# Weights and small parameters of a hybrid attention, S5, mLSTM and MoE layer laid out in the order of their tiles

## The chip, the cores and the metric

The kernel runs on one core of a Trainium2 chip. The metric is the device time of one execution in microseconds (us). The layouts of the inputs are made by numpy before the launch, and that is outside the time.

## The reference

One transformer-like layer with batch 1, 256 tokens and width 2048, all in float32. Shift, scale and gate vectors come from `silu(c) @ w_ada + b_ada`, a product of one row with a 2048 x 12288 matrix. The modulated, normalized input goes through `w_in` (2048 x 14344). The result is cut into the operands of three mixers (stick-breaking attention, an S5 state space layer, a chunkwise mLSTM) and their gates. Each mixer's output is projected, the gated sum goes through `w_out`, and after a second norm comes a mixture of 32 experts in 4 groups.

```python
mod = c_act @ w_ada[l] + b_ada[l]
h = modulate(rms_norm(x, norm_mix_g[l]), shift1, scale1)
proj = h @ w_in[l]
...
merged = jax.nn.sigmoid(g_sb) * (y_sb @ p_sb[l]) \
    + jax.nn.sigmoid(g_s5) * (y_s5 @ p_s5[l]) \
    + jax.nn.sigmoid(g_ml) * (y_ml @ p_ml[l])
x = x + gate1[:, None, :] * (merged @ w_out[l])
...
hid = jax.nn.silu(jnp.einsum('td,edf->tef', t, w1)) * jnp.einsum('td,edf->tef', t, w3)
y = jnp.einsum('tef,efd->td', hid * gates.astype(hid.dtype)[:, :, None], w2)
```

Of the experts each token uses two, but all 32 experts' matrices (2048 x 256 twice and 256 x 2048 each) are read. Some 480 MB are read in one execution, nearly all of them weights, each once.

## The kernel before

All weights are streamed through SBUF in tiles of 128 partitions by 2048 floats (1 MB, 8 KB per partition). Nearly all loads are issued from SP's queue.

**Start.** SP loads `c` (L94) and the two halves of `x` (L73); POOL loads the first constants (L96), the first part of `b_ada` (L98) and `norm_mix_g` (L100), both in pieces of four floats. `norm_x` (L366 on) normalizes `x` on ACT. `ada_pe(0)` (L309) streams the first eighth of the used part of `w_ada`: eight tiles, each of two transfers of 512 KB (L321, one for shift and one for scale, rows of 512 floats), multiplied on PE (L327) into `adarp`. The ring for these tiles has three buffers. Their sum becomes the shift and scale of the first 512 channels (`ada_cols`), with which `hT_block` makes the first modulated block hT; then the first matmuls of `w_in` (tile `u_w`) run.

**Early columns.** A loop over four blocks of 512 rows runs ten column chunks of `w_in` per block (u, sbq, sbk, sbv, mlq, mlk), while `ada_first` (L288) streams the next block's `w_ada` tiles, whose products DVE accumulates (L301, L303).

**Main part.** `ChanChunk` and `TokChunk` take a weight tile of 512 rows and 512 columns through `wsplit`: `load_raw` (L118, ring of three buffers) loads it, ACT rounds it to fp32r in two halves (L131), DVE makes the remainder (L132), and PE multiplies three times (`mm3`, L142 to L144). The order of the chunks is that of the program: the rest of `w_in` for the mixers, then its gate columns (g_sb, g_ml, g_s) alternating with the projections p_sb, p_ml, p_s5, then w_out. In the background DVE runs the S5 recurrence (L695 to L698) and the remaining two thirds of `w_ada` (`ada_rest`, L337; tile `adar`, also through L118; DVE L353). `rows4` and `rows_kp` (L252, L255) give the source of each tile: 4 rows of 2 KB per partition, either neighbouring ones or 128 rows apart.

**Experts.** A `Pair` (L1357 on) is two experts that share PE's columns, half 0 and half 1. `load_in` (L1372) loads for each of four blocks of 512 rows and each expert a tile with 4 KB of w1 and 4 KB of w3 per partition, in two transfers (L1377); `load_out` (L1383) loads w2 in tiles of 8 KB rows (L1391). The ring has eleven buffers. PE multiplies w1 and w3 into `h` and w2 into `y` (both L1397); between them come gathers of the next tokens (xg, xgT), the scatter of the last ones (sc), and for `h` a silu on ACT (L1409), a product on DVE (L1410) and a transpose.

Except in blocks marked `manual_schedule`, the framework writes each engine's queue when the kernel is built: by priority among the instructions that it takes to be ready. So the order in a queue can differ from the program's.

```python
def rows4(mat, c0):
    return lambda j: mat[512 * j:512 * j + 512, c0:c0 + 512].rearrange("(p k) c -> p k c", k=4)
...
for wi, nm in enumerate(("moe_w1", "moe_w3")):
    nc.sync.dma_start(out=raw[:, wi], in_=A[nm][e, 512 * j:512 * j + 512, :]
                      .rearrange("(p k) f -> p k f", k=4))
```

Of the kernel before, what the change touches and what calls it, by code (L numbers as in the profile page):

```python
# [10 lines left out]
F32 = mybir.dt.float32  # L11
# [7 lines left out]
P = 128  # L19
D = 2048  # L20
T = 256
W = 1024
NE = 32
FF = 256
# [4 lines left out]
CONST_COLS = 6 * 128 + 2 + 16 + 12  # L29
# [15 lines left out]
def kernel(ctx: ExitStack, tc: tile.TileContext, A, out, dbg=None):  # L45
# [43 lines left out]

    def cols4(v):  # L90
        return v.rearrange("(j p k) -> p j k", p=P, k=4)
# [9 lines left out]
    gmoe = cp.tile([P, 4, 4], F32, name="gmoe")  # L101
    ccol = cp.tile([P, 4, 4], F32, name="ccol")
# [185 lines left out]
    def ada_first(j):  # L288
        acc = pbp.tile([P, 2, 512], F32, tag="acc", bufs=1, name=f"acc{j}")
        for jr in range(4):  # L290
            for kp in range(2):
                raw = pap.tile([P, 2, 2, 512], F32, tag="raw", bufs=3, name=f"ada{j}_{jr}_{kp}")
                for v in range(2):
                    c0 = v * D + 512 * j
                    nc.sync.dma_start(out=raw[:, v], in_=A["w_ada"][512 * jr:512 * jr + 512, c0:c0 + 512]
                                      .rearrange("(p k) c -> p k c", k=4)[:, 2 * kp:2 * kp + 2, :])
                with tc.high_priority(120):
                    for q in range(2):
                        cs = ccol[:, jr, 2 * kp + q:2 * kp + q + 1]
                        if jr == 0 and kp == 0 and q == 0:  # L300
                            nc.vector.tensor_scalar(acc, raw[:, :, q], cs, None, op0=ALU.mult)  # L301
                        else:
                            nc.vector.scalar_tensor_tensor(acc, raw[:, :, q], cs, acc, op0=ALU.mult, op1=ALU.add)  # L303
                    if jr == 3 and kp == 1:
                        ada_cols(modc[:, 0:2, 4 * j:4 * j + 4], ball[:, j:j + 5:4, :],
                                 ada_rows([acc[:, v] for v in range(2)], f"f{j}"), f"f{j}")
                yield

    def ada_pe(j):  # L309
# [6 lines left out]
        for jr in range(4):  # L316
            for kp in range(2):
                raw = pap.tile([P, 2, 2, 512], F32, tag="raw", bufs=3, name=f"ada{j}_{jr}_{kp}")
                for v in range(2):
                    c0 = v * D + 512 * j  # L320
                    nc.sync.dma_start(out=raw[:, v], in_=A["w_ada"][512 * jr:512 * jr + 512, c0:c0 + 512]  # L321
                                      .rearrange("(p k) c -> p k c", k=4)[:, 2 * kp:2 * kp + 2, :])
                for kk in range(2):
# [13 lines left out]
    def ada_rest():  # L337
        cols = []
        for v in (2, 3, 4, 5):
            for half in range(2):  # L340
                acc = pbp.tile([P, 1024], F32, tag="acc", bufs=1, name=f"accr{v}_{half}")
                for n in range(16):
                    jr, kp, q = n // 4, n // 2 % 2, n % 2
                    if q == 0:
                        c0 = v * D + 1024 * half
# [63 lines left out]
    def s5_params():  # L409
# [114 lines left out]
        br, bi, ta, tb = (cut(512 * i, 32, 16) for i in range(4))  # L524
        nc.gpsimd.dma_start(out=br, in_=A["s5_b_re"].rearrange("(j g) p h -> (g p) j h", g=2))
        nc.gpsimd.dma_start(out=bi, in_=A["s5_b_im"].rearrange("(j g) p h -> (g p) j h", g=2))
        bc = cut(2048, 2, 32, 16)
# [41 lines left out]
        for r, nm in enumerate(("s5_c_re", "s5_c_im")):  # L569
            cc = cut(0, 8, 64)  # L570
            nc.gpsimd.dma_start(out=cc, in_=A[nm].rearrange("(u g) h p -> (g h) u p", g=8))
            cx = cut(512, 8, 2, 64)
# [173 lines left out]
    def gates_chunk():  # L746
        wif = pap.tile([P, 2, 2, 512], F32, tag="raw", bufs=3, name="wif")[:, 0, 0, :128].rearrange("p (k c) -> p k c", k=16)
        for j in range(4):
            nc.gpsimd.dma_start(out=wif[:, 4 * j:4 * j + 4, :],
                                in_=A["w_in"][512 * j:512 * j + 512, COL["gates"]:COL["gates"] + 8]  # L750
                                .rearrange("(p k) c -> p k c", k=4))
        ws = p1.tile([P, 2, T], F32R, tag="sby", name="wifs")
# [198 lines left out]
    for j in range(4):  # L951
# [12 lines left out]
        if j == 2:  # L964
            nc.sync.dma_start(out=cst[:, 256:], in_=A["consts"][:, 256:])
            nc.sync.dma_start(out=ball[:, 8:], in_=cols4(A["b_ada"])[:, 8:])
            nc.sync.dma_start(out=gmoe, in_=cols4(A["norm_moe_g"]))
        if j == 3:
# [393 lines left out]
    class Pair:  # L1362
# [220 lines left out]
    def overflow():  # L1583
# [3 lines left out]
        with tc.If(nmax > 64):  # L1587
# [9 lines left out]
            for tt in range(2):  # L1597
# [12 lines left out]
                for e in range(NE):  # L1610
                    ph = psum("ms", f"ho{tt}_{e}")
                    for j in range(4):
                        raw = st.tile([P, 2048], F32, tag="raw", bufs=3, name=f"o13_{tt}_{e}_{j}")
                        rv = raw.rearrange("p (w k f) -> p w k f", w=2, k=4)
                        for wi, nm in enumerate(("moe_w1", "moe_w3")):
                            nc.sync.dma_start(out=rv[:, wi], in_=A[nm][e, 512 * j:512 * j + 512, :]
                                              .rearrange("(p k) f -> p k f", k=4))
                        for kk in range(4):
# [136 lines left out]

_SHAPES = dict(
    x=(T, D), c=(D,), norm_mix_g=(D,), norm_moe_g=(D,), final_g=(D,), w_ada=(D, 6 * D), b_ada=(6 * D,),
    w_in=(D, 14344), ml_conv=(4, 2 * W), ml_i_bias=(4,), ml_f_bias=(4,), s5_lam_re=(64, 64), s5_lam_im=(64, 64),
    s5_log_dt=(64,), s5_b_re=(64, 64, 16), s5_b_im=(64, 64, 16), s5_c_re=(64, 16, 64), s5_c_im=(64, 16, 64),
    s5_d=(W,), s5_w_glu=(W, W), p_sb=(W, D), p_s5=(W, D), p_ml=(W, D), w_out=(D, D), moe_w_group=(D, 4),  # L1760
    moe_b_group=(4,), moe_w_router=(D, 32), moe_b_router=(32,), moe_w1=(NE, D, FF), moe_w3=(NE, D, FF),
    moe_w2=(NE, FF, D))

# [17 lines left out]
```

## Time and profile before

| | us |
|---|---|
| median of 3 runs | 1601.37 |
| lowest and highest | 1597.33, 1603.7 |
| profiled execution, its time | 1600.31 |
| span of its profile | 1598.5 |

The span runs from the first to the last instruction of the profiled execution; 1.81 us of that execution's time lie around it. By the profile's page the time falls into three stretches: a start without much matmul work up to about 40 us, the part from there to about 1093 us in which weights are split and multiplied, and the experts from 1093 us to about 1580 us. The page's engines are PE (matmul), PEld (weight load), DVE, ACT, POOL and SP. Busy time of PE includes modelled ends of pipelined matmuls, so what PE waits for says more than its share.

### The profile page before, as it was taken

To read this page: it belongs to the slowest core of one execution; us is meant where nothing else is said; L and a number is where in the kernel's file an instruction comes from. 1 tells how busy PE (TensorE), PEld (TensorE's weight loads), DVE (VectorE), ACT (ScalarE), POOL (GpSimd) and SP (SyncE) were. 2 spreads that over 40 slices of the span, in tenths; PEclk is the share of its full clock that TensorE was granted. 3 is DMA by queue.
4 is the path that set the end of the run, shared out by engine and by line. 5 is a ranking of instruction groups with operands and counts; after the bars stand their busy time and mean duration, and the time that the engine had idled before them with its cause. 6 is when DMAs were issued, how large, how long until landed. Compare 5 with 4: busy or idle time off the path is not lost.

```text
span 1598.5 us, 25021 instructions
## 1 busy us (share of the span) xinstructions
PE 1509.0 (94%) x10228; PEld 1140.2 (71%) x10228; DVE 1015.1 (64%) x1733; ACT 568.6 (36%) x755; POOL 39.0 (2%) x63
## 2 busy tenths in 40 slices
PE   4999999989999998999999999999999999999996
PEld 2999999888888988899999998874334433443332
DVE  0879997889879999999778866553213212222124
ACT  3554363774534333333444344342112111111112
POOL 1000010010000000000000010000000000000000
PEclk9999999999999999999999999999999999999998
DMA  9998967677787676777789976566999999999994
GB/s 343 386 348 305 319 191 222 220 223 261 247 300 265 229 264 231 273 264 264 263 308 327 318 267 241 207 228 257 414 413 412 413 402 374 412 392 411 404 412 183
DMA packets 172249, 488.13 MB, mean 305 GB/s; under 512 B 13876, under 2 KB 14048, under 8 KB 162784
## 3 DMA queue, kind: packets, MB, share of 16 engines
q1 hardware_dynamic: 168464, 473.27, 80.5%
q0 software_dynamic: 3088, 12.14, 2.3%
q8 instruction: 82, 1.34, 0.3%
q10 hardware_dynamic: 576, 1.05, 0.2%
q14 instruction: 39, 0.32, 0.1%
HBM read 479.06 MB, written 6.31 MB: 304 GB/s over the span
## 4 chain that ended last, share of the span: by engine, by line
PE 54%; DVE 25%; DMA 10%; issue 6%; ACT 4%; POOL 0%; SPq 0%; ACTq 0%; DVEq 0%; POOLq 0%
PE h L1397 14%; PE y L1397 9%; DVE accr L353 5%; DMA adar<-in_w_ada_dram 4%; DVE g_sb_w L132 2%; DVE g_ml_w L132 2%; PE sc L1446 2%; PE wo_b L143 2%; PE wo_b L144 2%; PE wo_b L142 2%; DVE bu L698 2%; PE xg L1312 2%; DVE s5pp L695 2%; DVE bu L697 1%; DVE s5qq L696 1%
## 5 line engine op out<-in xcount | busy, mean ns | idle before, releaser
L1397 PE MATMUL h<-w,XG 128*64 128x512 f32 x1024 | 245.3, 599 | 0.0
L1397 PEld LDWEIGHTS h<-w,XG 128*64 128x64 f32 x1024 | 75.7, 137 | 139.1 <-issue 137.4
L353 DVE SCALAR_TENSOR_TENSOR accr<-adar,ccol,accr 128x1024 f32<-128x1024 f32 x120 | 153.5, 1280 | 18.2 <-DMA adar<-in_w_ada_dram 17.3
L1397 PE MATMUL y<-w,hh 128*64 128x512 f32 x512 | 150.4, 598 | 0.5 <-ACT hh L1419 0.5
L1410 DVE SCALAR_TENSOR_TENSOR s<-h,gg,s 128x256 f32<-128x256 f32 x16 | 7.7, 484 | 167.8 <-ACT s L1409 167.8
L1455 DVE TENSOR_TENSOR x<-x,sc 128x512 f32<-128x512 f32 x64 | 43.0, 682 | 105.7 <-PE sc L1446 105.7
L1397 PEld LDWEIGHTS y<-w,hh 128*64 128x64 f32 x512 | 49.0, 136 | 81.5 <-issue 77.7
L1409 ACT ACTIVATE s<-h 128x256 f32<-128x256 f32 x16 | 6.1, 383 | 212.3 <-PE h L1397 212.3
L144 PE MATMUL g_sb_b<-hT,g_sb_w 128*128 128x256 f32 x256 | 73.1, 285 | 8.5 <-DVE g_sb_w L132 8.4
L144 PE MATMUL g_ml_b<-hT,g_ml_w 128*128 128x256 f32 x256 | 72.4, 283 | 3.3 <-DVE g_ml_w L132 3.3
L1287 DVE TENSOR_SCALAR XG<-xgT,G,modc 128x128 f32<-128x128 f32 x64 | 26.0, 410 | 77.0 <-ACT XG L1284 77.0
L144 PE MATMUL g_s_b<-hT,g_s_w 128*128 128x256 f32 x256 | 72.1, 282 | 1.6 <-DVE g_s_w L132 1.4
L142 PE MATMUL g_ml_b<-hT,g_ml_w 128*128 128x256 f32 x256 | 72.4, 283 | 0.0
L142 PE MATMUL g_sb_b<-hT,g_sb_w 128*128 128x256 f32 x256 | 71.9, 281 | 0.0
L142 PE MATMUL g_s_b<-hT,g_s_w 128*128 128x256 f32 x256 | 71.7, 280 | 0.0
L143 PE MATMUL g_s_b<-hT,g_s_w 128*128 128x256 f32 x256 | 71.6, 280 | 0.0
L143 PE MATMUL g_ml_b<-hT,g_ml_w 128*128 128x256 f32 x256 | 71.5, 279 | 0.0
L143 PE MATMUL g_sb_b<-hT,g_sb_w 128*128 128x256 f32 x256 | 71.4, 279 | 0.0
L132 DVE TENSOR_TENSOR wo_w<-wo_w,wo_w 128x1024 fp32r<-128x1024 f32 x32 | 39.0, 1223 | 31.8 <-ACT wo_w L131 31.6
L303 DVE SCALAR_TENSOR_TENSOR acc<-ada,ccol,acc 128x1024 f32<-128x1024 f32 x45 | 57.6, 1281 | 0.5
L131 ACT CAST g_ml_w<-g_ml_w 128x1024 fp32r<-128x1024 f32 x32 | 32.0, 1048 | 70.4 <-DMA g_ml_w<-in_w_in_dram 47.4
L144 PEld LDWEIGHTS g_sb_b<-hT,g_sb_w 128*128 128x128 f32 x256 | 48.1, 188 | 11.2 <-DVE g_sb_w L132 11.1
(506 smaller groups left out, 4361.7 us busy)
## 6 DMA issues: line engine op xcount, KB each, us to landing
w<-in_moe_w_dram SPq DMA_DIRECT2D x256, 512.0 KB, 9.2
adar<-in_w_ada_dram SPq DMA_DIRECT2D x64, 1024.0 KB, 5.5
w<-in_moe_w_dram SPq DMA_DIRECT2D x64, 1024.0 KB, 9.9
ada<-in_w_ada_dram SPq DMA_DIRECT2D x64, 512.0 KB, 7.5
g_sb_w<-in_w_in_dram SPq DMA_DIRECT2D x16, 1024.0 KB, 5.4
g_ml_w<-in_w_in_dram SPq DMA_DIRECT2D x16, 1024.0 KB, 5.4
g_s_w<-in_w_in_dram SPq DMA_DIRECT2D x16, 1024.0 KB, 6.1
wo_w<-in_w_out_dram SPq DMA_DIRECT2D x16, 1024.0 KB, 5.1
```

Source lines behind the costliest of these rows:

```text
L131: nc.scalar.copy(out=hv, in_=src)
L132: nc.vector.tensor_tensor(out=lv, in0=src, in1=hv.bitcast(F32), op=ALU.subtract)
L142: nc.tensor.matmul(o, lhsT=lhs[0], rhs=rhs[0], start=start, stop=False, **kw)
L143: nc.tensor.matmul(o, lhsT=lhs[0], rhs=rhs[1], start=False, stop=False, **kw)
L144: nc.tensor.matmul(o, lhsT=lhs[1], rhs=rhs[0], start=False, stop=stop, **kw)
L303: nc.vector.scalar_tensor_tensor(acc, raw[:, :, q], cs, acc, op0=ALU.mult, op1=ALU.add)
L353: nc.vector.scalar_tensor_tensor(acc, raw[:, q], cs, acc, op0=ALU.mult, op1=ALU.add)
L695: V.tensor_tensor(out=pp, in0=L2R, in1=prev, op=ALU.mult)
L698: V.tensor_tensor(out=cur, in0=cur, in1=qq, op=ALU.add)
L1312: nc.tensor.matmul(self.pt[j], lhsT=self.sel[:, tt], rhs=xs[i][:, tt, 512 * j:512 * j + 512], start=(i == 0 and tt == 0), stop=(i == 1 and ...
L1397: nc.tensor.matmul(o[sl, :], lhsT=lhsT[:, sl], rhs=rhs(h), start=start, stop=stop, tile_position=(0, 64 * h), skip_group_check=True)
L1455: V.tensor_tensor(out=x1[:, tt, sl], in0=x1[:, tt, sl], in1=pts[tt], op=ALU.add)
```

## The change

Numpy reorders the weights before the launch, so that each tile's 128 x 2048 floats lie in one piece of memory, 8 KB per partition. `w_in` loses its eight gate columns to an array of their own (`w_gates`, one transfer in place of four). A tile of `w_ada` for shift and scale, and a tile of w1 and w3, come in one transfer each in place of two. `c`, `norm_mix_g`, `b_ada` and `norm_moe_g` stand together in one array `vectors`: its first 64 columns come in one transfer on SP in place of one on SP and two on POOL, the rest in one in place of two. The S5 parameters b and c are laid out likewise. w2, `x` and the constants stay as they were. No instruction of PE, DVE or ACT is changed.

```diff
-    craw = cp.tile([P, 4, 4], F32, name="craw")
-    nc.sync.dma_start(out=craw, in_=cols4(A["c"]))
+    vec = cp.tile([P, 144], F32, name="vec")
+    craw, gmix, ball, gmoe = (vec[:, 4 * a:4 * b].rearrange("p (j k) -> p j k", k=4)
+                              for a, b in ((0, 4), (4, 8), (8, 32), (32, 36)))
+    nc.sync.dma_start(out=vec[:, :64], in_=A["vectors"][:, :64])
     x_load()
     nc.gpsimd.dma_start(out=cst[:, :256], in_=A["consts"][:, :256])
-    ball = cp.tile([P, 24, 4], F32, name="ball")
-    nc.gpsimd.dma_start(out=ball[:, :8], in_=cols4(A["b_ada"])[:, :8])
-    gmix = cp.tile([P, 4, 4], F32, name="gmix")
-    nc.gpsimd.dma_start(out=gmix, in_=cols4(A["norm_mix_g"]))
...
     def rows4(mat, c0):
-        return lambda j: mat[512 * j:512 * j + 512, c0:c0 + 512].rearrange("(p k) c -> p k c", k=4)
+        return lambda j: mat[(c0 - 8 * (c0 > 8192)) // 512, j].rearrange("p (k c) -> p k c", k=4)
 
     def rows_kp(mat, c0):
-        return lambda j: mat[512 * j:512 * j + 512, c0:c0 + 512].rearrange("(k p) c -> p k c", p=P)
+        return lambda j: mat[c0 // 512, j].rearrange("p (k c) -> p k c", k=4)
...
                 raw = pap.tile([P, 2, 2, 512], F32, tag="raw", bufs=3, name=f"ada{j}_{jr}_{kp}")
-                for v in range(2):
-                    c0 = v * D + 512 * j
-                    nc.sync.dma_start(out=raw[:, v], in_=A["w_ada"][512 * jr:512 * jr + 512, c0:c0 + 512]
-                                      .rearrange("(p k) c -> p k c", k=4)[:, 2 * kp:2 * kp + 2, :])
+                nc.sync.dma_start(out=raw.rearrange("p v k c -> p (v k c)"), in_=A["w_ada"][8 * j + 2 * jr + kp])
...
-                        raw = load_raw(A["w_ada"][512 * jr:512 * jr + 512, c0:c0 + 1024]
-                                       .rearrange("(p k) c -> p k c", k=4)[:, 2 * kp:2 * kp + 2, :],
+                        raw = load_raw(A["w_ada"][16 * v + 8 * half + 2 * jr + kp].rearrange("p (k c) -> p k c", k=2),
                                        (2, 1024), f"adar{v}_{half}_{jr}_{kp}")
...
-        nc.gpsimd.dma_start(out=br, in_=A["s5_b_re"].rearrange("(j g) p h -> (g p) j h", g=2))
+        nc.gpsimd.dma_start(out=br, in_=A["s5_b_re"].rearrange("p (j h) -> p j h", j=32))
...
-                raw = moe_raw(f"w13_{e}_{j}").rearrange("p (w k f) -> p w k f", w=2, k=4)
-                for wi, nm in enumerate(("moe_w1", "moe_w3")):
-                    nc.sync.dma_start(out=raw[:, wi], in_=A[nm][e, 512 * j:512 * j + 512, :]
-                                      .rearrange("(p k) f -> p k f", k=4))
-                self.raw[j].append(raw)
+                raw = moe_raw(f"w13_{e}_{j}")
+                nc.sync.dma_start(out=raw, in_=A["moe_w13"][e, j])
+                self.raw[j].append(raw.rearrange("p (w k f) -> p w k f", w=2, k=4))
...
+    def tiles(m, order):
...
+        m = m.reshape(m.shape[-2:])
+        r, c = m.shape[0] // 512, m.shape[1] // 512
+        if order == "pk":
+            t = m.reshape(r, P, 4, c, 512).transpose(3, 0, 1, 2, 4)
+        else:
+            t = m.reshape(r, 4, P, c, 512).transpose(3, 0, 2, 1, 4)
+        return t.reshape(c, r, P, 2048)
...
+    ada = z["w_ada"].reshape(4, P, 2, 2, 6, D)
+    first = ada[..., :2, :].reshape(4, P, 2, 2, 2, 4, 512).transpose(5, 0, 2, 1, 4, 3, 6)
+    rest = ada[..., 2:, :].reshape(4, P, 2, 2, 4, 2, 1024).transpose(4, 5, 0, 2, 1, 3, 6)
+    a["w_ada"] = np.concatenate([first.reshape(32, P, 2048), rest.reshape(64, P, 2048)])
+    w13 = np.stack([z["moe_w1"].reshape(NE, 4, P, 4, FF), z["moe_w3"].reshape(NE, 4, P, 4, FF)], axis=3)
+    a["moe_w13"] = w13.reshape(NE, 4, P, 2048)
```

## Rows read from the trace of the kernel before

**Rows 1.** The page: busy us of each engine, share of the span, instructions.

```profile
PE 1509.0 (94%) x10228; PEld 1140.2 (71%) x10228; DVE 1015.1 (64%) x1733; ACT 568.6 (36%) x755; POOL 39.0 (2%) x63
```

**Rows 2.** Busy time by stretch; last three columns: granted clock, DMA share, GB/s.

```profile
24.00:40.00 16.00, 10.22 (x140) 5.45 (x140) 3.00 (x5) 3.20 (x5) 0.00 (x0) 0.89 1.03 378
460.00:740.00 280.00, 258.84 (x2125) 249.09 (x2125) 271.98 (x649) 96.66 (x104) 1.86 (x3) 1.00 0.74 258
1093.00:1560.00 467.00, 451.59 (x1900) 180.57 (x1901) 106.50 (x228) 75.97 (x151) 0.00 (x0) 1.00 1.00 400
1120.00:1200.00 80.00, 77.65 (x335) 30.03 (x332) 14.85 (x32) 12.84 (x26) 0.00 (x0) 1.00 1.02 413
```

**Rows 3.** Waits of PE from 40 to 1080 us: total, times, longest.

```profile
PE g_sb_b L144 <- DVE g_sb_w L132: 8.4, 12, 1.4
PE pp_sb_b L144 <- DVE pp_sb_w L132: 5.0, 7, 2.0
PE pp_ml_b L144 <- DVE pp_ml_w L132: 3.9, 4, 1.5
PE g_ml_b L144 <- DVE g_ml_w L132: 3.3, 4, 1.6
PE wo_b L143 <- DVE wo_w L132: 2.1, 1, 2.1
```

**Rows 4.** Waits of the issuing queue SP from 1120 to 1560 us.

```profile
SPq L1377 <- PE h L1397: 74.5, 45, 5.1
```

**Rows 5.** The tile w from 1120 to 1560 us: PE's idle time before it.

```profile
  DMA w<-in_moe_w_dram: 1.8, 6
```

**Rows 6.** The chain of waits, 0 to 42 us: start, us, what.

```profile
1.78 8.84 DMA x_sb<-in_x_dram
...
27.54 8.63 DMA ada<-in_w_ada_dram
...
41.91 0.58 PE u_b L143
```

**Rows 7.** Timeline of POOL, 0 to 12 us: start, us, instruction.

```profile
1.95 0.93 POOL L98 DMA_DIRECT2D ball<-in_b_ada_dram  x1
2.86 0.77 POOL L100 DMA_DIRECT2D gmix<-in_norm_mix_g_dram  x1
```

**Rows 8.** The tile x_sb: from issue to landing, two transfers.

```profile
DMA to landing us min/median/max: 5.4/7.1/8.8
```

**Rows 9.** Timeline of PE, 33 to 38 us: start, us, instruction.

```profile
33.51 2.04 PE L327 MATMUL adarp<-ada,c 128*32 128x128 f32 x32 [0.69 <-DMA ada<-in_w_ada_dram]
36.21 1.57 PE L327 MATMUL adarp<-ada,c 128*32 128x128 f32 x24 [0.66 <-DMA ada<-in_w_ada_dram]
```

**Rows 10.** Waits of ACT from 460 to 740 us.

```profile
ACT g_sb_w L131 <- DMA g_sb_w<-in_w_in_dram: 56.9, 15, 7.1
```

**Rows 11.** DMA issues: KB each, median us from issue to landing.

```profile
g_sb_w<-in_w_in_dram SPq DMA_DIRECT2D x16, 1024.0 KB, 5.4
...
wo_w<-in_w_out_dram SPq DMA_DIRECT2D x16, 1024.0 KB, 5.1
...
ymlr<-ymld SPq DMA_DIRECT2D x1, 1024.0 KB, 5.2
```

**Rows 12.** Timeline of ACT, 563 to 569 us.

```profile
564.28 2.00 ACT L131 CAST g_sb_w<-g_sb_w 128x1024 fp32r<-128x1024 f32 x2 [7.14 <-DMA g_sb_w<-in_w_in_dram]
```

**Rows 13.** Timeline of DVE, 563 to 569 us.

```profile
564.45 1.28 DVE L353 SCALAR_TENSOR_TENSOR accr<-adar,ccol,accr 128x1024 f32<-128x1024 f32 x1
...
566.14 1.22 DVE L132 TENSOR_TENSOR g_sb_w<-g_sb_w,g_sb_w 128x1024 fp32r<-128x1024 f32 x1
```

**Rows 14.** The chain of waits, 1113 to 1148 us.

```profile
1114.13 7.07 PE y L1397 x32
```

**Rows 15.** The chain of waits, 1195 to 1245 us.

```profile
1199.72 4.54 PE y L1397 x16
...
1219.88 10.50 PE h L1397 x48
```

More of the change, by code (lines that the diff above doesn't have):

```diff
@@ L318, in ada_pe @@
                 raw = pap.tile([P, 2, 2, 512], F32, tag="raw", bufs=3, name=f"ada{j}_{jr}_{kp}")
[L319 to L322, printed above, removed]
+                nc.sync.dma_start(out=raw.rearrange("p v k c -> p (v k c)"), in_=A["w_ada"][8 * j + 2 * jr + kp])
                 for kk in range(2):
@@ L344, in ada_rest @@
                     if q == 0:
-                        c0 = v * D + 1024 * half
-                        raw = load_raw(A["w_ada"][512 * jr:512 * jr + 512, c0:c0 + 1024]
-                                       .rearrange("(p k) c -> p k c", k=4)[:, 2 * kp:2 * kp + 2, :],
+                        raw = load_raw(A["w_ada"][16 * v + 8 * half + 2 * jr + kp].rearrange("p (k c) -> p k c", k=2),
                                        (2, 1024), f"adar{v}_{half}_{jr}_{kp}")
@@ L524, in s5_params @@
         br, bi, ta, tb = (cut(512 * i, 32, 16) for i in range(4))
-        nc.gpsimd.dma_start(out=br, in_=A["s5_b_re"].rearrange("(j g) p h -> (g p) j h", g=2))
-        nc.gpsimd.dma_start(out=bi, in_=A["s5_b_im"].rearrange("(j g) p h -> (g p) j h", g=2))
+        nc.gpsimd.dma_start(out=br, in_=A["s5_b_re"].rearrange("p (j h) -> p j h", j=32))
+        nc.gpsimd.dma_start(out=bi, in_=A["s5_b_im"].rearrange("p (j h) -> p j h", j=32))
         bc = cut(2048, 2, 32, 16)
@@ L570, in s5_params @@
             cc = cut(0, 8, 64)
-            nc.gpsimd.dma_start(out=cc, in_=A[nm].rearrange("(u g) h p -> (g h) u p", g=8))
+            nc.gpsimd.dma_start(out=cc, in_=A[nm].rearrange("p (u q) -> p u q", u=8))
             cx = cut(512, 8, 2, 64)
@@ L747, in gates_chunk @@
         wif = pap.tile([P, 2, 2, 512], F32, tag="raw", bufs=3, name="wif")[:, 0, 0, :128].rearrange("p (k c) -> p k c", k=16)
[L748 to L751, printed above, removed]
+        nc.gpsimd.dma_start(out=wif, in_=A["w_gates"].rearrange("p (k c) -> p k c", k=16))
         ws = p1.tile([P, 2, T], F32R, tag="sby", name="wifs")
@@ L965 @@
             nc.sync.dma_start(out=cst[:, 256:], in_=A["consts"][:, 256:])
-            nc.sync.dma_start(out=ball[:, 8:], in_=cols4(A["b_ada"])[:, 8:])
-            nc.sync.dma_start(out=gmoe, in_=cols4(A["norm_moe_g"]))
+            nc.sync.dma_start(out=vec[:, 64:], in_=A["vectors"][:, 64:])
         if j == 3:
@@ L1614, in overflow @@
                         rv = raw.rearrange("p (w k f) -> p w k f", w=2, k=4)
-                        for wi, nm in enumerate(("moe_w1", "moe_w3")):
-                            nc.sync.dma_start(out=rv[:, wi], in_=A[nm][e, 512 * j:512 * j + 512, :]
-                                              .rearrange("(p k) f -> p k f", k=4))
+                        nc.sync.dma_start(out=raw, in_=A["moe_w13"][e, j])
                         for kk in range(4):
@@ L1753, with laid_out @@
     overflow()
[L1756 to L1762, printed above, removed]
+def laid_out(inputs):
+    z = {k: np.asarray(v, np.float32) for k, v in inputs.items()}
+    a = {k: z[k].reshape(s) for k, s in _PLAIN.items()}
+    def tiles(m, order):
[6 more added lines that the diff above has]
+        return t.reshape(c, r, P, 2048)
+    w_in = z["w_in"].reshape(D, -1)
+    g0 = COL["gates"]
+    a["w_in"] = tiles(np.concatenate([w_in[:, :g0], w_in[:, g0 + 8:]], axis=1), "pk")
+    a["w_gates"] = w_in[:, g0:g0 + 8].reshape(4, P, 4, 8).transpose(1, 0, 2, 3).reshape(P, 128)
+    for nm in ("p_sb", "p_s5", "p_ml", "w_out", "s5_w_glu"):
+        a[nm] = tiles(z[nm], "kp")
+    ada = z["w_ada"].reshape(4, P, 2, 2, 6, D)
[4 more added lines that the diff above has]
+    a["moe_w13"] = w13.reshape(NE, 4, P, 2048)
+    for nm in ("s5_b_re", "s5_b_im"):
+        a[nm] = z[nm].reshape(32, P, 16).transpose(1, 0, 2).reshape(P, 512)
+    for nm in ("s5_c_re", "s5_c_im"):
+        a[nm] = z[nm].reshape(8, P, 64).transpose(1, 0, 2).reshape(P, 512)
+    cols = [z[nm].reshape(-1, P, 4).transpose(1, 0, 2).reshape(P, -1)
+            for nm in ("c", "norm_mix_g", "b_ada", "norm_moe_g")]
+    a["vectors"] = np.concatenate(cols, axis=1)
+    a["consts"] = const_array()
+    return {k: np.ascontiguousarray(v, np.float32) for k, v in a.items()}
@@ L1765 @@
+_PLAIN = dict(
+    x=(T, D), final_g=(D,), ml_conv=(4, 2 * W), ml_i_bias=(4,), ml_f_bias=(4,), s5_lam_re=(64, 64),
+    s5_lam_im=(64, 64), s5_log_dt=(64,), s5_d=(W,), moe_w_group=(D, 4), moe_b_group=(4,), moe_w_router=(D, 32),
+    moe_b_router=(32,), moe_w2=(NE, FF, D))
 def kernel(**inputs):
@@ L1770 @@
     arrays, args = {}, {}
-    for name, shape in list(_SHAPES.items()) + [("consts", (P, CONST_COLS))]:
-        a = const_array() if name == "consts" else np.ascontiguousarray(inputs[name]).reshape(shape)
+    for name, a in laid_out(inputs).items():
         arrays[f"in_{name}_dram"] = a
```

3 lines of the change are left out of this document (removed).

## The prediction

> **What bounds the kernel now.** I read the page first. PE is busy for 94% of the span and no other engine for more than 71% [rows 1]. A share over the whole span mixes stages, so next comes the table of stretches [rows 2]. Three things are to be seen in it. From 24 to 40 us PE is busy for 10.22 of 16 us while the DMA share is 1.03: there the transfers set the pace, at 378 GB/s. From 460 to 740 us DVE is busy for 271.98 of 280 us and the DMA share is only 0.74. From 1093 to 1560 us PE is busy for 451.59 of 467 us and the DMA share is 1.00, so both could be the bound.
>
> Which of them it is, the waits tell. In the long middle part PE waits for weight tiles that DVE has yet to split, 8.4 + 5.0 + 3.9 + 3.3 = 20.6 us in 27 waits, which all fall between 460 and 740 us; outside that stretch the longest such wait is 2.1 us [rows 3]. Among the experts SP's queue waits 74.5 us for PE to free buffers of w1 and w3 [rows 4], and PE itself waits 1.8 us in all for their data [rows 5]. So PE is the bound there, with the DMA close behind. In short, the weights' transfers are on the path in the first 40 us; in the middle they are late by tenths of a microsecond at a time; among the experts they are hidden.
>
> **The start.** The path runs through the second half of x, which lands at 1.78 + 8.84 = 10.62 us, and the last tile of w_ada, which lands at 27.54 + 8.63 = 36.17 us; the modulated matmuls run freely from 41.91 us [rows 6]. Between the two landings nine tiles arrive, eight of w_ada and one of w_in. Three terms:
>
> - *Longer rows.* A tile of 1.049 MB takes 2.774 us at the 378 GB/s of these 2 KB rows and 2.539 us at the 413 GB/s that the experts' rows of 4 and 8 KB reach when the DMA is full [rows 2]. The difference is 0.235 us, and nine tiles make 2.1 us. The same table gives the lower bound: if the 378 is the stage and not the row, 0.
> - *The small parameters.* POOL issues b_ada and norm_mix_g at 1.95 and 2.86 us, in pieces of 16 bytes [rows 7]. The first half of x lands 5.4 us after an issue at 1.24, so at 6.6 us, and the second, with the same 1 MB, 4.0 us later [rows 8, 6]. At 413 GB/s 2.54 us would do. The 1.4 us between them bound what the small pieces took; no row shows them taking it, so the other end is 0. I take 1.2, because nothing else new is queued between the two halves. The new transfer on SP ahead of x replaces one that stood in the same place. What hides behind b_ada is nothing before 38 us.
> - *One transfer in place of two.* PE could begin a tile of w_ada when its first half had landed. Behind the last landing stood 24 records of 32, 1.57 us; a whole tile takes 2.04 us [rows 9]. That costs 0.5 us.
>
> Sum: 2.1 + 1.2 - 0.5 = 2.8 us gained, with ends at a loss of 0.5 and a gain of 3.5. What is late next is PE, which from 42 us hardly waits.
>
> By the Trainium skill, "DMA: Bandwidth & Descriptors", section Specifications, a transfer needs only pieces of 512 bytes to run at line rate, so rows of 2 KB would already have it; the first term would be 0 and the start would gain 0.7 us. The trace speaks against it, 378 beside 413 GB/s at a full DMA share, though in different stages.
>
> **The middle, 42 to 1093 us.** Every tile of w_in, the projections and w_out changes from four rows of 2 KB per partition to one of 8 KB, the background tiles of w_ada from two of 4 KB. What counts is how long a tile takes from issue to landing, because the ring has three buffers and ACT waits 56.9 us, 15 times, for tiles of g_sb to land [rows 10]. Today a tile of w_in takes 5.4 us, one of w_out with the same rows 5.1, and the one 8 KB row transfer of that size on SP without much traffic, ymlr, 5.2 [rows 11]. So a lone transfer gains 0.2 to 0.3 us, and one behind another gains 0.235 more from the first's shorter stream. Taking 0.3 for each of the 27 waits gives 8.1 us. DVE limits this: it is idle for only 280 - 271.98 = 8.0 us of that stretch [rows 2], and many waits are its own. At 564.28 us ACT starts on a tile just landed, its first half is done after 1.0 us, and DVE comes to it at 566.14, because of a product for w_ada and recurrence steps before it [rows 12, 13]. I take half, 4 us, and 1 us for all waits outside the stretch. The ends are 0, if DVE takes it all back, and 20.6 + 2.1 = 22.7 us, if every wait vanishes. The transfers of the S5 parameters and of the gate columns lie on POOL's queue beside matmuls that do not wait for them: 0. If that cover were gone, each is 256 KB or less, a quarter of the 5 us tile.
>
> **The experts and the end.** Two transfers of 512 KB become one of 1 MB; both halves are needed by the first matmul anyway. PE's 1.8 us of waiting [rows 5] bound the gain; I take 0. The cover is PE: at 413 GB/s the 467 x 400 GB/s = 187 MB of this stretch need 452 us, about PE's own 451.59 [rows 2], so a faster PE would find the DMA next. Nothing of the end is changed: 0.
>
> **Sum.** 2.8 + 4 + 1 = 7.8 us. The profiled execution took 1600.31 us (span 1598.5 and 1.81 around it), so **1592.5 us**. That execution is 1.06 us, 0.07%, below the median of 1601.37. About 0.5%, 8 us, is what a measurement of this kernel can tell from no change; against the median the border of faster is 1593.4.
>
> **The rivals.**
>
> *Nothing arrives.* The row length does not matter, or DVE and the stage swallow it; what is left is 0 to 3 us. For it: DVE's 97% in the stretch with most waits [rows 2], and the 5.2 us of ymlr [rows 11]. Against it: the start, where PE waits for DMA alone. Time 1600. The rule of the Trainium skill quoted above ("DMA: Bandwidth & Descriptors", Specifications) would give this too.
>
> *The experts' queue order gets better.* In the first pairs 32 matmuls of y take 7.07 us, 3.54 per 16 [rows 14]. Later the first 16 take 4.54, while h runs at 10.50 per 48, 3.50 per 16 [rows 15]. So in y the halves of PE's columns do not run side by side for 1.0 us. The queue is written from what is taken to be ready; fewer and longer transfers may change that. The row of 4.54 or 4.55 stands in 12 pairs of the chain, and the second block of y is at least as long: 2 x 12 = 24 us less, 1568. Against it: w2's own transfers are not changed.
>
> *The order gets worse (the other side).* The same mechanism at w1 and w3: one expert's tile now counts as ready only when all of its 1 MB is there, and its half of h is put a step behind. Today no block of h has this delay [rows 15]. If two of the four blocks of h in 13 pairs get 1.0 us each, 26 us are lost: 1592.5 + 26 = 1618. It decides from 1.3 us per pair, 17 us in all.
>
> **How the numbers follow.** The forecast has a chance of 0.55, nothing 0.15, the better order 0.18, the worse 0.12. The forecast's own range is 1585 to 1600, from DVE's 8 us of idle time given wholly and the start's better end to nothing. A little over half of it, 0.30, lies below 1593.4. Faster: 0.30 + 0.18 = 0.48. Same: 0.25 + 0.15 = 0.40. Slower: 0.12. The range reaches down to 1567, so that it holds a full better order, and up to 1606; the worse order is left out, and some 0.06 below for orders and middle gains together.
>
> **What the profile would show.** Right: matmuls of `u_b` run freely from about 39 us; x's second half lands before 9.5 us; the stretch from 24 us runs near 410 GB/s; ACT's and PE's waits for splits shrink by a third while DVE's stay; the experts take as long as before, 467 us, with larger leads of the data. Wrong: y blocks of 3.5 us or h blocks over 3.6 would say that the queue's order decided; a DMA rate still near 380 would sink the first term; a middle part shorter by over 10 us would say that DVE was not the limit I took it for.

## The result and the profile after

The kernel after takes 1593.48 us (median of 5 runs, 1589.71 to 1595.88) beside 1601.37 us before (5 runs); the ratio is 0.995 with a 95% interval of 0.9927 to 0.9973. The profiled execution took 1593.40 us, its span is 1591.6 us. The forecast was 1592.5 us. It had put the border at which a gain can be told from no change at 1593.4: the total lies on that border, so what the change does is read from the stages below.

The windows of the kernel after (columns as in [rows 2]: PE, PEld, DVE, ACT, POOL busy us, granted clock, DMA share, GB/s), with one stretch more, from 16 to 24 us:

```profile
16.00:24.00 8.00, 7.29 (x118) 4.48 (x114) 0.00 (x0) 2.00 (x3) 0.00 (x0) 1.00 0.94 356
24.00:40.00 16.00, 8.95 (x128) 5.22 (x116) 4.34 (x8) 4.62 (x8) 0.00 (x0) 0.89 1.01 420
460.00:740.00 280.00, 261.22 (x2139) 251.89 (x2138) 273.76 (x654) 98.82 (x107) 1.87 (x3) 0.99 0.71 260
...
1120.00:1200.00 80.00, 77.65 (x330) 30.87 (x327) 16.99 (x38) 14.68 (x30) 0.00 (x0) 1.00 1.01 422
```

Where the DMA is full it now moves 420 and 422 GB/s in place of 378 and 413 [rows 2]. Yet from 16 to 24 us the share is 0.94 and the rate 356: there it runs dry for a time.

The chain of waits of the kernel after, 0 to 42 us (start, us, what), answers to [rows 6]:

```profile
1.66 7.43 DMA x_sb<-in_x_dram
...
25.02 9.27 DMA ada<-in_w_ada_dram
...
40.50 0.39 PE u_b L137
```

The second half of x lands at 9.09 us (before 10.62), the last tile of w_ada at 34.29 (36.17), and u_b runs freely from 40.50 (41.91). So x is 1.53 us earlier and the start as a whole only 1.41.

PE's waits from 40 to 1080 us after (total, times, longest), beside [rows 3]:

```profile
PE g_sb_b L138 <- DVE g_sb_w L126: 7.1, 10, 1.5
PE pp_sb_b L138 <- DVE pp_sb_w L126: 4.6, 7, 1.7
PE g_ml_b L138 <- DVE g_ml_w L126: 3.7, 5, 1.8
PE pp_ml_b L138 <- DVE pp_ml_w L126: 3.2, 4, 1.4
PE wo_b L137 <- DVE wo_w L126: 2.1, 1, 2.1
```

The first four are 18.6 us in 26 waits, before 20.6 in 27. The DMA issues after, from 40 to 1080 us (KB each, median us from issue to landing), beside [rows 11]:

```profile
g_sb_w<-in_w_in_dram SPq DMA_DIRECT2D x16, 1024.0 KB, 4.9
...
wo_w<-in_w_out_dram SPq DMA_DIRECT2D x16, 1024.0 KB, 4.8
```

A tile of g_sb takes 0.5 us less, one of w_out 0.3. In the experts the chain of waits shows the same pieces as [rows 15]:

```profile
1276.35 10.50 PE h L1377 x48
...
1288.74 4.55 PE y L1377 x16
```

Between the first h blocks of two pairs in a row lie 30.88 and 32.35 us in turn, in both kernels. PE's instruction queue in the two kernels differs in two places, both in the first products of w_ada, and nowhere after them. From g_sb to w_out the queues of ACT and DVE, too, hold the same work in the same order in before, after, e2 and e4.

For the middle, the lengths of four stages are read from PE's timeline in each run: first matmul of u_b to first of g_sb, from there to the last of pp_ml, to the first of w_out, to the first of the experts. In us:

| kernel | u_b to g_sb | to end of pp_ml | to w_out | to experts | experts begin at |
|---|---|---|---|---|---|
| before | 438.4 | 347.1 | 143.4 | 124.4 | 1093.0 |
| mean of five with short rows (before, e1, e3, e4, e6) | 438.07 | 347.24 | 142.70 | 124.44 | |
| after | 438.2 | 344.2 | 139.7 | 125.9 | 1086.3 |
| mean of five with 8 KB rows (after, e2, e5, e7, e11) | 437.61 | 344.47 | 139.75 | 125.66 | |

Within five, one stage differs by 0.7 to 3.5 us from run to run. The change gains 2.8 us between 478 and 825 us and 3.0 us between 825 and 968 us, and 1.2 us go again while w_out starts. PE's idle time agrees for the larger part: in the first of these stages it is 19.7 to 21.7 us in the five with short rows and 18.3 to 19.3 in the five with 8 KB rows (means 20.7 and 18.8), in the second 1.2 to 2.5 us and none in all five (means 1.9 and 0). So 1.9 us of each gain are waits that PE no longer has; some 1 us of each is not found in its waits. What goes again is seen in the windows of after: for 3.5 us the granted clock is 0.53, close to the lower of its two levels (1.2 of 2.4 GHz), where before it was 1.00 in the like place.

```profile
960.00:964.00 4.00, 1.95 (x11) 1.38 (x10) 3.97 (x5) 1.05 (x1) 0.00 (x0) 0.99 0.00 0
964.00:967.50 3.50, 3.50 (x10) 2.69 (x10) 1.85 (x3) 0.50 (x1) 0.00 (x0) 0.53 0.61 225
```

In both kernels PE had just waited 2.1 us for the first split of w_out. The clock falls there in all five kernels with 8 KB rows, and in e6 alone of the other five. Why it falls after this wait in one and not in the other stays open.

### The profile page after: what moved, and what is told of

It is laid out like the page before. It is cut to its first block, busy times and chain, and to the rows that moved or that the text cites. A ratio compares the mean times of both kernels' runs of the same rounds, so it can differ in the third digit from the quotient of the medians.

```text
span 1591.6 us, 24728 instructions
## 1 busy us (share of the span) xinstructions
PE 1507.1 (95%) x10228; PEld 1139.9 (72%) x10228; DVE 1014.5 (64%) x1733; ACT 570.3 (36%) x755; POOL 31.7 (2%) x58
## 3 DMA queue, kind: packets, MB, share of 16 engines
q10 hardware_dynamic: 576, 1.05, 0.2%
## 4 chain that ended last, share of the span: by engine, by line
PE 69%; DVE 22%; ACT 4%; DMA 2%; issue 2%; SPq 0%; DVEq 0%; ACTq 0%
PE h L1377 14%; PE y L1377 9%; DVE accr L339 3%; DVE g_sb_w L126 2%; PE sc L1426 2%; DVE bu L684 2%; PE g_s_b L136 2%; PE wo_b L137 2%; PE g_s_b L137 2%; PE wo_b L138 2%; PE g_s_b L138 2%; PE wo_b L136 2%; DVE g_ml_w L126 2%; DVE s5pp L681 2%; PE xg L1294 2%
## 5 line engine op out<-in xcount | busy, mean ns | idle before, releaser
L125 ACT CAST wo_w<-wo_w 128x1024 fp32r<-128x1024 f32 x32 | 33.6, 1051 | 59.2 <-PE wo_b L138 46.1
```

The costliest lines, as they stand in the source:

```text
L125: nc.scalar.copy(out=hv, in_=src)
```

## The experiments

Each kernel was compared with runs of the kernel before on the same chip.

### Which part, and is it the row? (e1 to e4)

e1, e2 and e3 each make one part of the change on the kernel before. e4 keeps the whole change but for the row:

```diff
-            t = m.reshape(r, P, 4, c, 512).transpose(3, 0, 1, 2, 4)
+            t = m.reshape(r, P, 4, c, 512).transpose(3, 0, 2, 1, 4)
...
-        return t.reshape(c, r, P, 2048)
+        return t.reshape(c, r, 4, P, 512)
...
-        return lambda j: mat[c0 // 512, j].rearrange("p (k c) -> p k c", k=4)
+        return lambda j: mat[c0 // 512, j].rearrange("k p c -> p k c")
```

**e1, the start alone.** 

> The kernel before with two parts of the change only: the small parameters in one array (one transfer on SP in place of one on SP and two on POOL) and the first third of w_ada in single transfers with 8 KB per partition. All else is read as before. Forecast, from its own terms: eight of nine longer tiles give 8 x 0.235 = 1.9 us, the small parameters 1.2, the one transfer in place of two takes 0.5: the matmuls of u_b run freely 2.6 us earlier than 41.9 and the experts begin 2.6 us earlier than 1093.0; the ratio is about 0.998. If the rows of 2 KB were no hindrance, only the small parameters and the one transfer count: 0.7 us, and the stretch from 24 to 40 us would stay near 378 GB/s. If the whole change's gain sat in the start, the ratio would be 0.995.

Measured: 1598.92 us, ratio 0.9998 (0.9985 to 1.0011). u_b runs freely from 40.61 us, 1.30 us earlier than before, not 2.6.

**e2, the middle alone.** 

> The kernel before with the layouts of the middle part only: w_in, the projections, w_out, the glu matrix and the last two thirds of w_ada with 8 KB per partition in a row, the gate columns and the S5 parameters likewise. The start's small parameters and first tiles of w_ada, and w1 and w3, are as before. Forecast: the start gains 0.2 us (only its one tile of w_in is new), the middle some 5 us, so the experts begin at about 1088 us in place of 1093.0 and the ratio is 0.997. If DVE takes everything back in the stretch from 460 to 740 us, the experts begin at 1092.5 to 1093 and the ratio is 1.000.

Measured: 1592.40 us, ratio 0.9959 (0.9944 to 0.9975), 6.5 us less than before. The experts begin at 1086.3 us, though u_b began no earlier. Most of the change's gain is here.

**e3, the experts alone.** 

> The kernel before with one part of the change only: a tile of w1 and w3 in one transfer of 1 MB with 8 KB per partition in place of two of 512 KB. Forecast: PE is the bound of the experts and its queue is in the same order, so nothing: 0 us, within 1 us, though the DMA rate between 1120 and 1200 us goes from 413 to about 420 GB/s and the data lead by more. If the experts were held by the DMA, up to 467 x (1 - 413 / 420) = 8 us less, a ratio of 0.995; if halves of h had to wait for whole tiles, blocks of h over 3.6 us and up to 26 us more, 1.016.

Measured: 1602.38 us, ratio 1.0017 (1.0007 to 1.0028). The DMA's rate from 1120 to 1200 us is 421 GB/s. In its profile the experts up to the last scatter matmul take 488.8 us, before 490.5, and blocks of y and h are as before; the difference lies in the first 3.5 us of the experts, which run at a granted clock of 0.53 in before and 1.00 in e3. So the part gains nothing, as forecast; the 2.7 us more in its ten runs are not found in that one execution, which at 1597.37 us was the fastest of them, and stay open. By the totals the three parts add up to 0.3 + 6.5 - 2.7 = 4.1 us, where the whole change gives 8.0 (4.3 to 11.7). Each part is known to some 2 us, so this is no contradiction, but the totals alone do not divide the gain.

**e4, the whole change with rows of 2 KB.** 

> The kernel after, with every part of the change kept (each tile in one piece of 1 MB, one transfer where there were two, the small parameters in one array), except for the row: within that piece a partition's 8 KB stand in four separate rows of 2 KB as before (two of 4 KB for the last two thirds of w_ada, two of 4 KB for w1 and w3). If it is the length of the rows that made transfers shorter, the gain goes again but for the small parameters' 1.2 us less 0.5 us: ratio to before 0.9985 to 1.000, the stretch from 24 to 40 us near 380 GB/s, a tile of g_sb in 5.4 us from issue to landing, and the experts begin at about 1092. If it is that a tile lies in one place of memory, or that there are fewer transfers, it is as the kernel after: ratio 0.995, 420 GB/s, 4.9 us, 1086.3.

Measured: 1598.97 us, ratio 0.9997 (0.9983 to 1.0011). The window and the DMA issue of e4:

```profile
24.00:40.00 16.00, 9.07 (x136) 5.63 (x137) 2.69 (x4) 2.34 (x4) 0.00 (x0) 0.79 1.04 387
```

```profile
g_sb_w<-in_w_in_dram SPq DMA_DIRECT2D x16, 1024.0 KB, 5.4
```

387 GB/s at a full DMA, near the 378 of before, and 5.4 us for a tile, as before. The queues are in the order of the kernel after, the tiles lie in one place, and there are as few transfers; only the row differs. So the length of the row carries the gain. The chain of waits of e4 in the start:

```profile
1.66 7.78 DMA x_sb<-in_x_dram
...
27.87 8.73 DMA ada<-in_w_ada_first_dram
...
42.78 0.46 PE u_b L137
```

The second half of x lands at 9.44 us, with the small parameters in one array: 1.18 us before the 10.62 of before, against the 1.2 forecast. But u_b runs freely only from 42.78 us, 0.87 later than before, where 0.7 earlier was forecast: from x's second half to the last tile of w_ada it takes 36.60 - 9.44 = 27.16 us, before 25.55. One transfer per tile in place of two costs 1.6 us here that the forecast did not have; e7 shows why.

The traces' DMA packets give the size of the row's effect: a packet of 2 KB takes 84 ns at the median, one of 4 KB 159, one of 8 KB 310, as if each packet cost some 8.5 ns beside its bytes. The Trainium skill, "DMA: Bandwidth & Descriptors", section Specifications, names 512 bytes as the least for line rate. By the runs here, from 24 to 40 us 366 to 387 GB/s at 2 KB and 419 to 421 at 8 KB, the rate still grows beyond that.

### The start: does the ring run dry? (e7)

```diff
+                n = 2 * jr + kp
+                if n == 3:
+                    raw = st.tile([P, 2, 2, 512], F32, tag="raw", name=f"ada{j}_{jr}_{kp}")
+                elif n in (4, 5):
+                    raw = hlp.tile([P, 2, 2, 512], F32, tag="hl", bufs=4, name=f"ada{j}_{jr}_{kp}")
```

> The kernel after with six buffers in place of three for the first eight tiles of w_ada (three more from rings that are idle at that time). The same transfers and products. If the start's longer rows gave less than forecast because the ring runs dry (356 GB/s at a DMA share of 0.94 from 16 to 24 us), this stretch goes to about 415 GB/s and the last tile lands 0.9 to 2.8 us before 34.3, u_b runs freely at 37.7 to 39.6; the ratio is that of after less 0.001. If what is missing is the wait for one late DMA engine per tile (first engine at 32.06, last at 34.29 us), the landing stays within 0.3 us of 34.3.

Measured: 1590.72 us, ratio 0.9939 (0.9923 to 0.9955). Window and chain of e7:

```profile
16.00:24.00 8.00, 8.00 (x132) 5.09 (x129) 0.00 (x0) 2.34 (x3) 0.00 (x0) 1.00 1.01 418
```

```profile
1.66 7.78 DMA x_sb<-in_x_dram
...
17.95 14.89 DMA ada<-in_w_ada_dram
...
39.04 0.39 PE u_b L137
```

The dry stretch is full, 418 GB/s. From x's second half to the last tile of w_ada it is 32.84 - 9.44 = 23.40 us, in after 34.29 - 9.09 = 25.20, before 36.17 - 10.62 = 25.55. The landings of the nine tiles in the traces tell rows and buffers apart (us):

| kernel | rows, transfers per tile, buffers | from tile to tile at a full queue | nine such steps | measured | more than nine steps |
|---|---|---|---|---|---|
| before | 2 KB, two, three | 2.71 | 24.4 | 25.55 | 1.2 |
| e4 | 2 KB, one, three | 2.70 | 24.3 | 27.16 | 2.9 |
| after | 8 KB, one, three | 2.48 | 22.3 | 25.20 | 2.9 |
| e7 | 8 KB, one, six | 2.49 | 22.4 | 23.40 | 1.0 |

The longer rows give 0.22 us per tile, 1.96 us from e4 to after, close to the 2.1 forecast. With three buffers the one transfer per tile costs 1.7 us by this count, because SP issues the next tile only when a whole buffer is free; with six this is gone. In after the two nearly cancel, 0.35 us in all. The 1.0 us that e7 still takes more come with one tile, which lands at 25.38 us, 1.2 late (see the last section). u_b begins in e7 1.46 us before the kernel after.

### The experts: what would PE's order and the DMA be worth? (e5, e6)

```diff
-        for c in range(4):
-            cur.mm_out(0, c, py)
+        with tc.manual_schedule(engines={ENG.PE}):
+            for c in range(4):
+                cur.mm_out(0, c, py)
```

and the same for the second block of y.

**e5, on the kernel after.** 

> The kernel after, and PE's queue is written by hand within each block of y, so that the two experts' halves of PE's columns stand in turn (half 0, half 1, half 0, ...). The same matmuls, no other change. If PE alone is the bound of the experts, each block of 16 falls from 3.97 and 4.83 us to the 3.06 of the first pairs: 0.9 + 1.8 us in 12 pairs, about 30 us, so 1563 and a ratio of 0.977. If the DMA is close behind, as the prediction says: 187 MB at 422 GB/s need 443 of the 467 us, so at most 24 us, about 1570 and 0.981, and PE then waits for data of w1 and w3. If the halves' turn is not what makes these blocks long: 1593, 0.995.

**e6, on the kernel before.** 

> The kernel before with the same order of y by hand as in e5. This tells whether the change's part in the experts is worth nothing in itself or only because PE is the bound there. If the DMA then bounds: 187 MB at 413 GB/s need 452 of 467 us, so 15 us are gained, 1586 and a ratio of 0.991, and the change's experts are worth 9 us on top of its 8 elsewhere once PE is out of the way. If PE alone is the bound in both kernels: 30 us, 1571 and 0.981, the same step as in e5.

Measured: e5 1580.88 us, ratio 0.9871 (0.9852 to 0.9890), 12.6 us below after. e6 1587.88 us, 0.9928 (0.9909 to 0.9947), some 12 us below before. The second block of y in the chain of waits, with the next two matmuls of h, of after and of e5:

```profile
1294.89 4.06 PE y L1377 x13
...
1299.44 0.80 PE y L1377 x2
```

```profile
1293.23 3.58 PE y L1377 x16
1296.81 0.85 PE h L1377 x2
```

In after these 18 matmuls end at 1300.24, after 5.35 us; in e5 they take 4.43, so 0.9 less. The first block of 16, 4.55 us in after, gains nothing: in e5 it stands in two rows of 1.05 and 3.58 us, with transposes and scatters between them. So one block per pair gains, not two, and two pairs in a row take 61.36 us in place of 63.23, 1.9 less and not 4. Both kernels gain the same step, so PE bounds the experts in both even then. The slack is smaller in e6, though. The tile w of e6, PE's idle time before it from 1120 to 1560 us:

```profile
  DMA w<-in_moe_w_dram: 3.9, 11
```

Before, it was 1.8 us in 6 waits [rows 5]; in e5 there is no such row. The change's part in the experts is worth nothing as long as PE needs its data more slowly than 413 GB/s bring them; these 3.9 us are the first sign that it could begin to count.

### The middle: DVE's load or DVE's queue? (e8 to e10, e12)

**e8, fewer products of w_ada in the S5 stretch.**

```diff
-    rate = dict(s5=.75, fast=.8, slow=.55, a=0.0, b=0.0)
+    rate = dict(s5=.75, fast=1.0, slow=.3, a=0.0, b=0.0)
```

> The kernel after with the background products of w_ada on DVE put off: while the S5 recurrence runs their rate is 0.3 in place of 0.55 per step, afterwards 1.0 in place of 0.8, so that some 20 of the 44 in the stretch from 460 to 740 us (1.28 us each, 26 us of DVE) come later, where DVE is busy for 70% or less. If DVE is what limits the middle, PE's 27 stalls of 0.25 us and more between 460 and 740 us (24 us) shrink by half, 10 to 12 us less in all, 1582 and a ratio of 0.988. If the stalls come from the landing of the tiles, they stay and the time stays at 1593, 0.995. If the products put off come together before w_out, some of the gain is lost there.

Measured: 1614.37 us, ratio 1.0093 (1.0075 to 1.0112): slower, by 21 us against after. Window, and PE's waits from 40 to 1080 us, of e8:

```profile
460.00:740.00 280.00, 256.79 (x2072) 244.70 (x2071) 258.64 (x643) 101.70 (x109) 1.65 (x3) 1.00 0.62 225
```

```profile
PE g_sb_b L138 <- DVE g_sb_w L126: 9.9, 17, 1.7
PE g_ml_b L138 <- DVE g_ml_w L126: 7.2, 10, 2.5
PE pp_sb_b L138 <- DVE pp_sb_w L126: 5.8, 12, 0.6
```

DVE is busy for 15 us less, and PE waits more. The framework filled the gaps with S5 instructions: between two other instructions of DVE from g_sb to pp_ml stand 6.9 of them in a row on average, in after 4.9. So the edit changed the order as much as the load. And the products put off held up w_out: from the end of pp_ml to w_out it takes 148.9 us, in after 139.7. As a test of the load alone it failed. e9 was meant to leave the queue's places alone.

**e9 and e10, the same products an eighth as wide, after and before.**

```diff
-                        nc.vector.scalar_tensor_tensor(acc, raw[:, q], cs, acc, op0=ALU.mult, op1=ALU.add)
+                        nc.vector.scalar_tensor_tensor(acc[:, :128], raw[:, q, :128], cs, acc[:, :128], op0=ALU.mult,
+                                                       op1=ALU.add)
```

> The kernel after, where the background products of w_ada on DVE (after the first of each 16) cover 128 of their 1024 columns: the tiles are loaded as before, but 120 instructions fall from 1.28 us to about a quarter, some 40 us of DVE less between 460 and 740 us, in the places of the queue where they stood. It leaves out seven eighths of these sums, so gate, shift and scale of the second norm are not the real ones. If the load of DVE makes PE's stalls in that stretch (24 us in 29), they fall below a third and the experts begin 15 us or more before 1086.3. If the order in DVE's queue makes them (S5 steps ahead of splits, as e8 suggests), most of the stalls stay and the experts begin within 8 us of 1086.3. The time of the experts' part does not count here, only where it begins.

> The same edit on the kernel before; it too leaves out seven eighths of these sums. If DVE swallowed half of the change's gain in the middle, as the prediction has it, the two layouts now stand further apart than in the whole kernels: the experts begin 12 to 20 us later than in e9, where before and after differ by 6.7. If the landings matter only at the few tiles for which ACT is waiting, as the stalls of after from 825 us on suggest, the distance stays at 5 to 8 us.

Measured: e9 1595.34 us, 0.9970 (0.9957 to 0.9982), e10 1595.91 us, 0.9979 (0.9967 to 0.9992). The experts begin at 1089.0 and 1089.1 us. Window, and PE's waits from 440 to 1080 us, of e9:

```profile
460.00:740.00 280.00, 262.32 (x2123) 252.13 (x2122) 240.70 (x665) 100.19 (x107) 1.87 (x3) 0.99 0.72 263
```

```profile
PE g_sb_b L138 <- DVE g_sb_w L126: 10.6, 13, 2.1
PE pp_sb_b L138 <- DVE pp_sb_w L126: 3.5, 8, 0.6
PE g_ml_b L138 <- DVE g_ml_w L126: 2.6, 6, 0.6
...
PE pp_ml_b L138 <- DVE pp_ml_w L126: 0.8, 1, 0.8
```

DVE works 33 us less in the stretch, and PE still waits 17.5 us in 28 waits (after: 18.6 in 26). But the traces show that the products did not keep their places, as the expectation assumed: the framework rewrote DVE's queue for the shorter instructions, and S5 instructions now stand 6.5 in a row on average. So e9, like e8, changed load and order together and does not tell them apart. It does show that time DVE has to spare (39 us of idle time from 460 to 740 us) does not by itself shorten PE's waits.

What stands between is read from the traces. For the 26 waits of after, from the end of ACT's rounding to the start of the split on DVE, 55.4 us pass in all: 38 of them go to S5 instructions, 12 to products, 8 to other splits (the records overlap a little), and DVE is idle for 0.1. In e9 it is 100.2 us, 83 of them S5. If each split of after had started at once, some 11 of the 18.6 us of waiting would be gone; the rest stems from tiles that were late before DVE's turn.

Both forecasts for e10 missed: with light products the two layouts do not stand further apart, nor as far as in the whole kernels, but begin the experts at the same time. In part that is chance, as e9 loses 4.4 us to e10 before g_sb (440.7 and 436.3). From there on e9 and e10 have the same queues, and the distance is 347.0 - 346.2 = 0.8 us up to the end of pp_ml and 140.6 - 139.6 = 1.0 up to w_out, in the means of five 2.8 and 3.0. PE's idle time up to the end of pp_ml is 17.7 us in e9 and 17.9 in e10. It fits this that a DVE with spare time hides the longer landings of 2 KB rows and a loaded one passes them on to PE; with one execution of each, and another order of the queue, it is not shown.

**e12, the S5 recurrence on POOL** (on top of e11, below).

```diff
-            V.tensor_tensor(out=pp, in0=L2R, in1=prev, op=ALU.mult)
+            nc.gpsimd.tensor_tensor(out=pp, in0=L2R, in1=prev, op=ALU.mult)
...
```

and likewise the other three instructions of a step.

> The kernel of e11, and the S5 recurrence (127 steps of four small instructions, 0.27 to 0.28 us each on DVE, 138 us in all) runs on POOL, which is busy for 2 of the 280 us from 460 to 740 us. PE's queue is in the same order. It tells what makes PE's stalls there (25 us in 31 in e11), after e9 has shown that the load of the w_ada products does not. If it is the steps that stand ahead of the splits in DVE's queue, the stalls fall to 10 us or less and the experts begin 12 to 20 us before the 1085.6 of e11: 1561 to 1569, a ratio to before of 0.976 to 0.981. If it is the landing of the tiles, nothing changes: 1580.6, 0.988. The risk lies in POOL's speed: a copy of 128x64 takes 0.38 us there, at which the chain ends near 650 us, long before PE needs it at about 740; from 0.55 us per instruction on, PE waits for the chain and loses 5 us for each 0.01 us more.

Measured: 1622.02 us, ratio 1.0123 (1.0098 to 1.0148): 41 us slower than e11. PE's waits of e12 from 440 to 1080 us:

```profile
PE g_sb_b L138 <- DVE g_sb_w L126: 58.4, 2, 41.4
```

Two waits, 58.4 us, are more than the whole loss, and one of 0.6 us for a tile of pp_sb is what is left of the rest: in e11 these tiles made 18.0 us in 26 waits. The two long ones come from what stands on POOL's queue behind the recurrence, two transfers (ymld, issued at 538.91 and 566.07 us, in e11 at 490.55 and 498.39). DVE waits 45.5 us for the first.

So PE's waits there come with the S5 steps on DVE: without them they are gone but for 0.6 us. e12 takes away the steps' load (138 us) together with their places, and DVE is idle for 122 us of the stretch, so by itself it does not separate the two either. That it is what stands ahead of the splits rather than DVE's share is read from the trace of after and from e9's idle time; how much another order alone would gain was not tried, nor was a version with the two transfers on another queue. The price of POOL was also misjudged. Its timeline in e12, while DVE is idle and while DVE works:

```profile
458.25 0.37 POOL L690 TENSOR_TENSOR bu<-bu,s5qq 128x64 f32<-128x64 f32 x1
...
459.01 1.34 POOL L688 TENSOR_TENSOR s5qq<-L2I,bu 128x64 f32<-128x64 f32 x1
```

and DVE's beside it:

```profile
458.73 2.72 DVE L345 SCALAR_TENSOR_TENSOR accr<-adar,ccol,accr 128x1024 f32<-128x1024 f32 x2 [1.50 <-DMA adar<-in_w_ada_dram]
```

The mean over the chain is 0.60 to 0.63 us per instruction, and DVE's splits of g_sb rise from 1217 to 1354 ns. The Trainium skill, "GPSIMD Engine Reference", section 1, Specifications, says that POOL shares its SBUF interfaces with DVE, with contention where DVE reads two inputs from SBUF; the trace agrees, as the product reads two.

### Both gains together (e11)

The edits of e5 and e7 in one kernel.

> The kernel after with the two edits that gained on the chip: y's halves in turn (e5, 12.6 us less than after) and six buffers for the first eight tiles of w_ada (e7, 2 to 3 us less than after). They lie in different stages, so the sum: 1593.5 - 12.6 - 2 = 1579, a ratio to before of 0.986. If one undoes the other, as a faster start could let the experts' DMA fall behind, 0.987 or more.

Measured: 1580.58 us (1579.45 to 1582.21), ratio 0.9879 (0.9862 to 0.9895), so 19 us below the kernel before and 13 below after. Nearly all of it is the order of y; that the start's 1.5 us add to it can't be read from the total. With e5 it is the fastest of all that ran.

## Why the prediction was right, and where it was not

The time was right, 1593.48 us beside 1592.5. The largest term, the middle, has the right size, though not for the reason given; the start came out at half, because one of its terms left out a cost. By the stages of the traces the change gains 1.4 + 5.0 = 6.4 us, by the totals 8.0 (4.3 to 11.7). So it is in part luck that the total meets the forecast to 1 us.

- *The start*, 2.8 us forecast, 1.4 measured. "The small parameters" is right: 1.2 forecast, and x's second half lands 1.18 us earlier in e4 and e7, 1.46 in e1 and 1.53 in after. "Longer rows" is right as well: 2.1 forecast, 1.96 between e4 and after. "One transfer in place of two" is the step that failed. It was put at 0.5 us, for what PE has left behind the last landing, and that came: 2.03 us, before 1.57 [rows 9]. But the same step also lengthens the landings, by 1.6 us (27.16 in e4, 25.55 before), which the prediction put at nothing: the ring has three buffers, and a transfer now frees or fills a whole one. e7 with six buffers takes this cost away. Of the signs named, x's landing (9.09 us) and the rate (420 GB/s) came; u_b at about 39 us came only in e7.
- *The middle*, 5 us forecast, 5.0 between the means of five. The cap "DVE limits this" was argued from its 8.0 us of idle time. Idle time is not the cap: in e9, with another order of its queue, DVE has 39 us of it and the waits stay. In after the larger part of the waits comes from what stands ahead of the splits in DVE's queue, most of it S5 steps, which no landing changes, and so they did not shrink by a third but from 20.6 to 18.6 us. The 4 us that the forecast put into 460 to 740 us are 2.8 over the longer stretch to 825. Outside stands more than the 1 us forecast: 3.0 us before w_out, where PE's waits for g_s and pp_s go. In before, PE's waits from 825 to 969 us were these, in after none is listed:

```profile
PE pp_s_b L143 <- DVE ys L739: 1.2, 1, 1.2
PE g_s_b L144 <- DVE g_s_w L132: 0.9, 2, 0.6
```

  The errors cancelled: right in sum, wrong in place and in part in cause. DVE's waits for tiles of w_ada (from 460 to 970 us 16.0 us before, 10.3 after) are no clear part of it: the five with short rows have 14.0 to 18.8 us, the five with 8 KB rows 10.3 to 15.1. How the gain divides between PE's tiles and those of w_ada was not tried by itself.
- *The experts*, 0 forecast. Right: the trace shows the same blocks, and e6 shows that PE is the bound even with 12 us less work.
- *Rivals.* "Nothing arrives" is ruled out by e2 and e4. The two of the queue's order did not happen, as PE's order among the experts is unchanged. The price of the better order, 24 us, was twice too high: e5 gains 12.6, because one block of y per pair gets shorter and not two.

## What to carry to other kernels

Give a streamed tile the longest row the layout allows, since 2 KB rows cost 8 to 10% of the DMA's rate here, but expect the gain only where something waits for a landing. When two transfers become one, count the ring's buffers again: issue waits for a whole tile. A busy engine's share does not tell whether its load or the order of its queue makes others wait. An edit that shortens its work can have the framework write another queue, as here; so compare the order of the queue in the two traces before reading the result.

## What the runs showed beside

- From about 22 us on one DMA engine lags in the start: in after 15 of the 16 have landed the last tile of w_ada at 32.69 us and the last one at 34.29. In e7 all 16 land a tile of w_ada within 0.4 us up to 21.66 us; with the next, at 25.38, one is 1.26 behind. Between them, at 22.16 us, one packet of 16 KB on the instruction queue starts and takes 1.10 us. Such a packet stands there in before (21.97 us, 1.07 us), where the lag of the next tile is 1.4, and in after (22.50 us, 0.96 us), where the tile that lands at 26.84 has 1.6. The trace does not name a packet's engine, so that it makes the lag is likely but not shown; the lag is as large as the whole gain of the start.
- An instruction on POOL takes 0.37 us beside an idle DVE and 1.2 to 1.4 us beside one that works (e12).
- The mean granted clock differs between executions of one kernel: by a fit within each of before, after and e1 to e4, 0.001 of it goes with 0.86 us. That is part of the scatter that hides differences of a microsecond or two in these totals; the stages of the traces tell more.
